# Logits in the order of use, mixing of x behind the store of a head's output, the last output tile in two halves, side copies first: a hybrid decoder layer on one core

## The chip, the cores and the metric

The kernel runs on one core of a Trainium2 chip. The metric is the device time of one execution in microseconds (us), taken as the median of several runs. Beside it stands one execution recorded by the hardware profiler, from which the profile's numbers come.

## The reference

A decoder layer over 512 positions plus 16 learned meta positions, model width 2048. One input projection gives queries, keys and values of 8 attention heads (128 wide each) and the three inputs b, c, u of a gated short convolution (1024 channels). The two groups are normalized, projected together and added to the residual; then comes a SwiGLU feed-forward part of width 5632.

```python
n = _rmsnorm(h, g_mix[l])
p = n @ w_in[l]
q, k, v, gb, gc, u = jnp.split(p, ...)
q = _rmsnorm(q.reshape(b, L, N_ATTN_HEADS, HEAD_DIM), g_q[l])
k = _rmsnorm(k.reshape(b, L, N_ATTN_HEADS, HEAD_DIM), g_k[l])
o_attn = _stick_breaking_attention(q, k, v)
o_conv = gb * _causal_dwconv(gc * u, conv_w[l])
o = jnp.concatenate([_rmsnorm(o_attn, ...), _rmsnorm(o_conv, ...)], axis=-1)
h = h + o @ w_out[l]
n2 = _rmsnorm(h, g_ffn[l])
h = h + (jax.nn.silu(n2 @ w_gate[l]) * (n2 @ w_up[l])) @ w_down[l]
```

Stick-breaking attention takes, for query t and key s, the weight beta[t,s] times the product of (1 − beta[t,j]) over the keys j between s and t, with beta = sigmoid(q·k/√128). In log space that is a reverse cumulative sum over the keys.

## The kernel before

**Products.** Every product is done in split numbers. A weight tile of 128 × 1024 is loaded into `sw_in` by the load queue of SyncE, its rounded part `hi` is cast by ScalarE (ACT, L202) and the rest `lo` is subtracted by VectorE (DVE, L203), both into one of three rotating buffers of `sw_split`. The activations are split the same way. Each product is then three matmuls on TensorE (PE): `hi·ah`, `hi·al`, `lo·ah` (L311 to L313 in the heads, L772 to L774 in the output projection, L793 to L795 in the convolution, gate/up and down).

**Stages by the span's time.** 0 to 43: start and split of x. 43 to 390: eight heads of about 42.6 us, each with the products of v, q and k. 390 to 640: products of the convolution group. 640 to 774: output projection, 16 tiles of 128 output channels over 512 positions, each with a part from attention (bank x) and a part from the convolution (bank z). 774 to 1617: 44 pairs of gate/up. 1617 to 2045: down projection.

**Work hung on the products.** A head's attention is issued in pieces between the products of the next head, by a count of finished weight steps: `after(n, work)`. `attend` makes the transposes of v (`va`, `vb`, L548 and L549), the logits z for three blocks of keys (`z_0`, `z_1`, `z_2`, L563 to L565, with two small fp32 products L568 and L569 for the last keys in `z_2`), and their logarithms on ACT and DVE (L590 to L594), with causal selects on GpSimd (POOL, L581). The sums over later keys follow in the order block 2, 1, 0 (`sums`, tiles `c`, L618 to L624; `sph`/`spl` and `bh`/`bl` are the split operands). `mix` multiplies the weights by v into `o`, writes o's split into a stage tile `st_o` (L655 and L656) and stores it by POOL's queue (L658), and adds o² to `acc_a` (L343 and L344). Small PSUM tiles (`va`, `vb`, z, c, the norms' sums) come from one pool of four banks; stage tiles from a pool of two.

`mix_x` prepares data for the convolution part: of x, loaded as four position blocks, it makes sums and differences (L477 to L482), splits them into two stage tiles `st_x` (L324) and stores them (L486). It is issued once a head, behind the split of the head's query.

**Pairs.** The convolution group, gate/up and down multiply pairs of weight tiles with position halves by a scheme of seven block products instead of eight (`pair_product`): banks x, z, y, and side copies `p1`, `p5`, `u2` of banks on ACT (L813, L815, L817) that free the bank for the next block. Sums of weight tiles for the mixed products are made on DVE (L209, L219, L252). For gate/up, the activations' mixes `f` and their splits are made from `src` behind the output tiles (`mixed_blocks`, L980 to L987). The first gate/up pair starts with the y block.

**Order.** The order of the instructions of each engine is set by a list scheduler in the order of the program text, with priorities (`high_priority`) and explicit constraints (`issue_after`, `keep_in_program_order`).

Of the kernel before, what the change touches and what calls it, by code (L numbers as in the profile page):

```python
# [15 lines left out]
P = 128  # L16
# [17 lines left out]
def hybrid_layer(ctx: ExitStack, tc: tile.TileContext, xT, w_in, w_out, w_gu, w_down, vecs, out):  # L34
# [291 lines left out]
    def rsqrt(dst, v, n, y=None, t=None, eng=ve, times=None):  # L326

        y = t512(n, "r", 3) if y is None else y
        t = t512(n, "r", 3) if t is None else t
        sc.activation(y[:, :n], v, AF.Ln)  # L330
        sc.activation(y[:, :n], y[:, :n], AF.Exp, scale=-0.5)
        sc.activation(t[:, :n], y[:, :n], AF.Square)
        if times is not None:
            eng.tensor_tensor(y[:, :n], y[:, :n], times, ALU.mult)
        eng.scalar_tensor_tensor(t[:, :n], t[:, :n], -0.5, v, ALU.mult, ALU.mult)
        eng.scalar_tensor_tensor(dst, t[:, :n], 1.5, y[:, :n], ALU.add, ALU.mult)

    def square_sum(acc, src, first, s=None, eng=gp):
# [148 lines left out]

    def qk_norm(read, dst, parts_of, name, then=None):

# [6 lines left out]
        def finish():  # L496
# [19 lines left out]
    def head(h):  # L516
# [27 lines left out]
    def attend(h, kn, kh, kl, qn, qh, ql, vt):  # L544
# [12 lines left out]

        zs = []
        for b in range(3):
            z = small(f"z{h}_{b}")  # L560
            kk, q0 = slice(b * P, (b + 1) * P), Q0[b]
# [3 lines left out]
            pe.matmul(z[:, :n], kl[:, kk], qh[:, q0:], start=False, stop=True)  # L565
# [77 lines left out]
        def mix(ws):  # L643
# [10 lines left out]
            st = stage(f"st_o{h}")[:, : 2 * SEQ].rearrange("p (a b) -> p a b", a=2)  # L654
            sc.activation(st[:, 0], o, AF.Copy, scale=g)  # L655
            ve.scalar_tensor_tensor(st[:, 1], o, g, st[:, 0].bitcast(F32), ALU.mult, ALU.subtract)  # L656
            square_sum(acc_a, o, h == 0)
            gp.dma_start(oa_dram[h], st)  # L658

        after(14, lambda: sums(2))  # L660
# [4 lines left out]
    def token_scale(acc, dst, count, name, work, eng=ve, in_order=False):  # L665
# [11 lines left out]
        ve.tensor_scalar(v, ps, 1.0 / count, EPS, ALU.mult, ALU.add)  # L677
        rsqrt(dst, v, SEQ, y, t, eng)

# [87 lines left out]

    def wide_product(ps, acts):
        hi, lo = next_w()
        for n, (k, ah, al) in enumerate(acts):  # L770
            kk = slice(k * P, (k + 1) * P)
            pe.matmul(ps, hi[:, kk], ah, start=n == 0, stop=False)  # L772
            pe.matmul(ps, hi[:, kk], al, start=False, stop=False)
            pe.matmul(ps, lo[:, kk], ah, start=False, stop=n == 7)  # L774
            tick()

# [20 lines left out]
    def pair_product(acts, cols, out2, side, fourth=None):  # L797
# [14 lines left out]
        block_product(x, acts[0], True)  # L812
        sc.copy(p1, x)  # L813
        block_product(z, acts[1], True)
        sc.copy(p5, z)  # L815
        block_product(x, acts[2], False)
        sc.copy(u2, x)  # L817
        block_product(z, acts[3], False)
# [100 lines left out]
    def out_tile():  # L919
        i = len(ps_out)  # L920
        ps_out.append([xyz.tile([P, 512], F32, tag=t, name=f"po{i}{t}") for t in ("x", "z")])

# [6 lines left out]
    for i, j in enumerate(OUT_TILES):  # L929
# [40 lines left out]
        def residual(eng):  # L970
            ve.tensor_tensor(t1, ps[0], acc_a, ALU.mult)
            eng.tensor_tensor(hj, hj, t1, ALU.add)
            ve.tensor_tensor(t2, ps[1], acc_c, ALU.mult)
            eng.tensor_tensor(hj, hj, t2, ALU.add)
            sc.activation(src[:, 2 * half : 2 * half + 2], two(hj), AF.Copy, scale=g_ffn[:, j : j + 1])

        def split_f(s, i):
            split(acts[s][:, 0, k], acts[s][:, 1, k], src[:, i])

        def mixed_blocks():  # L980
            split_f(0, 0)
            ve.tensor_tensor(src[:, 4], src[:, 3], src[:, 1], ALU.subtract)
            split_f(1, 4)
            ve.scalar_tensor_tensor(src[:, 4], src[:, 4], -1.0, src[:, 0], ALU.mult, ALU.subtract)
# [247 lines left out]
```

## Time and profile before

| | |
|---|---|
| runs | 2044.81, 2046.19, 2046.81 us; median 2046.19 |
| profiled execution | 2046.62 us, of which 2044.8 are the span |
| busy: PE, DVE, ACT, POOL | 2027.8, 1728.4, 1074.9, 349.3 us |
| mean granted clock of PE | 0.999 |
| matmuls on PE | 16134 |

A row of the timeline gives start, duration, engine, line, operation, output and input tiles, shape, number, and in square brackets the idle time ahead of it with what ended it. A row of the waits gives the engine and tile that waited, what for, the total, the number of times and the longest. A row of the stages gives their bounds and length, the busy time and the number of instructions of PE, PEld (weight loads), DVE, ACT and POOL, then the clock granted to PE (1 is full), the busy share of the DMA engines and their rate. "From start to start" means the time between two matmuls' starts, less what the same shape takes without a wait.

### The profile page before, as it was taken

How to read it: one execution, taken by the hardware profiler on the slowest of the kernel's cores; microseconds unless marked ns; L12 is line 12 of the kernel's file. 1: busy time of each engine (PE TensorE's matmuls, PEld its weight loads, DVE VectorE, ACT ScalarE, POOL GpSimd, SP SyncE). 2: the span in 40 equal slices, each digit the busy share in tenths (PEclk: the TensorE clock that was granted, in tenths of full speed). 3: DMA queues.
4: the chain of work that ended last, by engine and by line, in shares of the span. 5: the costliest groups of instructions: out<-in, count | busy, mean ns of one | idle time of the engine just before them, and what ended most of it. 6: DMA issues, size and time to landing. Idle time of an engine off the chain costs nothing.

```text
span 2044.8 us, 39586 instructions
## 1 busy us (share of the span) xinstructions
PE 2027.8 (99%) x16134; PEld 1962.6 (96%) x16134; DVE 1728.4 (85%) x2187; ACT 1074.9 (53%) x1555; POOL 349.3 (17%) x514
## 2 busy tenths in 40 slices
PE   9999999999999999999999999999999999999999
PEld 8899999899998888999999999999999999999999
DVE  7877677698887778998988988988988978888887
ACT  7766667444454435555555554555555544444443
POOL 0111112200004441011111111111111242131211
PEclk9999999999999999999999999999999999999999
DMA  6343334732355555456465465455455899797764
GB/s 220 105 134 117 122 114 152 268 119 94 114 191 176 172 162 194 142 176 182 138 176 169 133 174 171 136 172 167 141 175 161 271 342 349 171 314 199 214 154 90
DMA packets 156086, 356.28 MB, mean 174 GB/s; under 512 B 13632, under 2 KB 67648, under 8 KB 155136
## 3 DMA queue, kind: packets, MB, share of 16 engines
q1 hardware_dynamic: 72208, 216.76, 32.6%
q0 software_dynamic: 83696, 136.99, 25.0%
q8 instruction: 126, 2.06, 0.4%
q14 instruction: 56, 0.46, 0.1%
HBM read 275.78 MB, written 77.92 MB: 173 GB/s over the span
## 4 chain that ended last, share of the span: by engine, by line
PE 89%; DVE 4%; ACT 2%; DMA 2%; issue 1%; POOL 1%; SPq 0%; DVEq 0%; ACTq 0%
PE x L793 13%; PE x L795 13%; PE x L794 13%; PE z L794 6%; PE z L795 6%; PE z L793 6%; PE y L795 3%; PE y L793 3%; PE y L794 3%; DVE sw_split L203 2%; PE pv L311 1%; PE pv L312 1%; PE pv L313 1%; PE pq L313 1%; PE pq L312 1%
## 5 line engine op out<-in xcount | busy, mean ns | idle before, releaser
L202 ACT CAST sw_split<-sw_in 128x1024 fp32r<-128x1024 f32 (+2 forms) x668 | 661.5, 992 | 712.1 <-PE z L794 189.0
L203 DVE TENSOR_TENSOR sw_split<-sw_in,sw_split 128x1024 fp32r<-128x1024 f32 (+2 forms) x668 | 778.0, 1165 | 150.2 <-ACT sw_split L202 144.7
L793 PE MATMUL x<-f,sw_split 128*128 128x256 f32 x1408 | 388.3, 276 | 2.9 <-ACT sides L813 1.9
L795 PE MATMUL x<-f,sw_split 128*128 128x256 f32 x1408 | 388.2, 276 | 0.6 <-DVE sw_split L203 0.6
L794 PE MATMUL x<-f,sw_split 128*128 128x256 f32 x1408 | 388.1, 276 | 0.0
L793 PEld LDWEIGHTS x<-f,sw_split 128*128 128x128 f32 x1408 | 265.0, 188 | 3.3 <-ACT sides L813 2.1
L795 PEld LDWEIGHTS x<-f,sw_split 128*128 128x128 f32 x1408 | 265.1, 188 | 1.0 <-DVE sw_split L203 1.0
L794 PEld LDWEIGHTS x<-f,sw_split 128*128 128x128 f32 x1408 | 265.1, 188 | 0.0
L1047 POOL DMA_DIRECT2D fd<-s x147 | 103.7, 922 | 713.7 <-DVE s L324 713.0
L209 DVE TENSOR_TENSOR sw_in<-sw_in 128x1024 f32<-128x1024 f32 (+1 forms) x164 | 187.9, 1146 | 11.5 <-DMA sw_in<-w_in 3.0
L793 PE MATMUL z<-f,sw_split 128*128 128x256 f32 x704 | 193.7, 275 | 0.3 <-ACT sides L815 0.3
L794 PE MATMUL z<-f,sw_split 128*128 128x256 f32 x704 | 193.6, 275 | 0.0
L795 PE MATMUL z<-f,sw_split 128*128 128x256 f32 x704 | 193.6, 275 | 0.0
L795 PE MATMUL x<-ring,sw_split 128*128 128x256 f32 x608 | 167.3, 275 | 0.4 <-DVE sw_split L203 0.4
L793 PE MATMUL x<-ring,sw_split 128*128 128x256 f32 x608 | 167.2, 275 | 0.0
L794 PE MATMUL x<-ring,sw_split 128*128 128x256 f32 x608 | 167.2, 275 | 0.0
L793 PEld LDWEIGHTS z<-f,sw_split 128*128 128x128 f32 x704 | 132.2, 188 | 0.5 <-ACT sides L815 0.5
L794 PEld LDWEIGHTS z<-f,sw_split 128*128 128x128 f32 x704 | 132.2, 188 | 0.0
L795 PEld LDWEIGHTS z<-f,sw_split 128*128 128x128 f32 x704 | 132.2, 188 | 0.0
L795 PEld LDWEIGHTS x<-ring,sw_split 128*128 128x128 f32 x608 | 114.1, 188 | 0.6 <-DVE sw_split L203 0.6
L794 PEld LDWEIGHTS x<-ring,sw_split 128*128 128x128 f32 x608 | 114.1, 188 | 0.0
L793 PEld LDWEIGHTS x<-ring,sw_split 128*128 128x128 f32 x608 | 114.1, 188 | 0.0
(604 smaller groups left out, 5459.2 us busy)
## 6 DMA issues: line engine op xcount, KB each, us to landing
sw_in<-w_gu SPq DMA_DIRECT2D x176, 512.0 KB, 3.9
sw_in<-w_in SPq DMA_DIRECT2D x92, 512.0 KB, 3.3
fd<-s POOLq DMA_DIRECT2D x147, 256.0 KB, 5.3
sw_in<-w_down SPq DMA_DIRECT2D x96, 384.0 KB, 4.2
ring<-fd POOLq DMA_DIRECT2D x42, 768.0 KB, 16.8
sw_in<-w_out SPq DMA_DIRECT2D x32, 512.0 KB, 3.4
out_T<-d POOLq DMA_DIRECT2D x54, 256.0 KB, 5.2
mix_dram<-st_x POOLq DMA_DIRECT2D x16, 516.0 KB, 4.0
```

The costliest lines, as they stand in the source:

```text
L202: sc.copy(hi, src)
L203: ve.tensor_tensor(lo, src, hi.bitcast(F32), ALU.subtract)
L209: return ve.tensor_tensor(sums[name], a, b, ALU.add)
L311: pe.matmul(ps, wh, ah[:, a:b], start=k + i == 0, stop=False)
L312: pe.matmul(ps, wh, al[:, a:b], start=False, stop=False)
L313: pe.matmul(ps, wl, ah[:, a:b], start=False, stop=k + i == last)
L793: pe.matmul(p, hi[:, kk], ah, start=start and j == k == 0, stop=False, skip_group_check=skip)
L794: pe.matmul(p, hi[:, kk], al, start=False, stop=False, skip_group_check=skip)
L795: pe.matmul(p, lo[:, kk], ah, start=False, stop=k == n - 1, skip_group_check=skip)
L1047: gp.dma_start(fd[c][s][:, :, k], t[:, :, i])
```

## The change

1. `attend` builds the logits in the order 2, 1, 0, in which `sums` uses them, the two fp32 products right behind z_2.
2. `mix_x` of a head is issued in `mix`, behind the split of the head's output, rather than behind the split of the next head's query. The add of o² to `acc_a` goes from POOL to DVE.
3. The convolution part of the last output tile is made in two halves of positions: 256 to 511 first in bank y, then 0 to 255 in bank z. Residual and mixes follow by halves; the square sum `acc_h` comes behind the last splits.
4. The side copies of the first two pairs of the convolution and of gate/up get the highest priority (`read_out`). The table for silu is loaded right behind the last square of the feed-forward norm.

```diff
-    def qk_norm(read, dst, parts_of, name, then=None):
+    def qk_norm(read, dst, parts_of, name):
...
-            last = split(hi, lo, dst[:, :n])
-            if then:
-                with tc.issue_after(last[0].ins), tc.issue_after(last[1].ins):
-                    then()
+            split(hi, lo, dst[:, :n])
...
-        after(9 if h else 22, qk_norm(read, qn, (qh, ql, SEQ), f"q{h}", (lambda: mix_x(h - 1)) if h else None))
+        after(9 if h else 22, qk_norm(read, qn, (qh, ql, SEQ), f"q{h}"))
...
-        zs = []
-        for b in range(3):
-            z = small(f"z{h}_{b}")
+        zs = {}
+        for b in (2, 1, 0):
+            zs[b] = z = small(f"z{h}_{b}")
...
-            zs.append(z)
-        z = zs[2]
-        pe.matmul(z[:, 272:416], kn[:, 384:512], qn[:, 368:], start=True, stop=True)
-        pe.matmul(z[:, 416:432], kn[:, 512:640], qn[:, 496:], start=True, stop=True)
+            if b == 2:
+                pe.matmul(z[:, 272:416], kn[:, 384:512], qn[:, 368:], start=True, stop=True)
+                pe.matmul(z[:, 416:432], kn[:, 512:640], qn[:, 496:], start=True, stop=True)
...
-            square_sum(acc_a, o, h == 0)
+            square_sum(acc_a, o, h == 0, eng=ve)
             gp.dma_start(oa_dram[h], st)
+            if h < HEADS - 1:
+                with tc.issue_after(hi.ins), tc.issue_after(lo.ins):
+                    mix_x(h)
...
-    def wide_product(ps, acts):
+    def wide_product(parts, acts):
         hi, lo = next_w()
-        for n, (k, ah, al) in enumerate(acts):
-            kk = slice(k * P, (k + 1) * P)
-            pe.matmul(ps, hi[:, kk], ah, start=n == 0, stop=False)
...
+        for ps, a, b in parts:
+            for n, (k, ah, al) in enumerate(acts):
+                kk = slice(k * P, (k + 1) * P)
+                pe.matmul(ps, hi[:, kk], ah[:, a:b], start=n == 0, stop=False)
...
+        def read_out(dst, src):
+            with tc.high_priority(1 << 20 if i in (CONV, CONV + 1) else 0):
+                sc.copy(dst, src)
...
-        sc.copy(p1, x)
+        read_out(p1, x)
...
+        if i == KT - 1:
+            z, y = ps_out[i][1][0][0], xyz.tile([P, 512], F32, tag="y", name=f"po{i}y")
+            ps_out[i][1] = [(y[:, T2:], T2, SEQ), (z[:, :T2], 0, T2)]
...
-            ve.tensor_tensor(t2, ps[1], acc_c, ALU.mult)
-            eng.tensor_tensor(hj, hj, t2, ALU.add)
-            sc.activation(src[:, 2 * half : 2 * half + 2], two(hj), AF.Copy, scale=g_ffn[:, j : j + 1])
+            for o, a, b in ps[1]:
+                ve.tensor_tensor(t2[:, a:b], o, acc_c[:, a:b], ALU.mult)
+                eng.tensor_tensor(hj[:, a:b], hj[:, a:b], t2[:, a:b], ALU.add)
+                blks = src[:, 2 * half + a // T2 : 2 * half + b // T2]
+                sc.activation(blks, hj[:, a:b].rearrange("p (a t) -> p a t", t=T2), AF.Copy, scale=g_ffn[:, j : j + 1])
+                if a:
+                    late_block()
...
+        def late_block():
+            ve.tensor_tensor(src[:, 4], src[:, 3], src[:, 1], ALU.subtract)
+            split_f(1, 4)
...
-                square_sum(acc_h, hj, False, wide_tmp("h", bufs=2), ve)
                 split_f(3, 5)
                 split_f(4, 1)
+                square_sum(acc_h, hj, False, wide_tmp("h", bufs=2), ve)
...
-            token_scale(acc_h, acc_h, D, "h", (w[:, 0], w[:, 1], a[:, 0], a[:, 1], b), ve, True)
+            last = token_scale(acc_h, acc_h, D, "h", (w[:, 0], w[:, 1], a[:, 0], a[:, 1], b), ve, True)
+            with tc.issue_after(last.ins):
+                sc.preload_act_table_set("silu_and_others")
```

Some line numbers shift: z's matmuls stand at L561 to L566 afterwards, the transposes at L546 and L547, the side copies all at L811, silu at L1078.

On PE, at the attention work of head 2 between two steps of k's product (`pk`), before:

```order
L548 MATMUL va_2097<-ident,tmp_2055 128x128 x4
L549 MATMUL vb_2098<-ident,tmp_2055 16x128
L563 MATMUL z_0_2111<-qh_1898,kh_1768 128x512
L564 MATMUL z_0_2111<-ql_1899,kh_1768 128x512
L565 MATMUL z_0_2111<-qh_1898,kl_1769 128x512
L311 MATMUL pk_2057<-n_132,sw_split 128x272
L563 MATMUL z_1_2115<-qh_1898,kh_1768 128x400
L564 MATMUL z_1_2115<-ql_1899,kh_1768 128x400
L565 MATMUL z_1_2115<-qh_1898,kl_1769 128x400
L312 MATMUL pk_2057<-n_132,sw_split 128x272
L313 MATMUL pk_2057<-n_132,sw_split 128x272
L563 MATMUL z_2_2119<-qh_1898,kh_1768 128x272
```

and afterwards:

```order
L546 MATMUL va_2097<-ident,tmp_2055 128x128 x4
L547 MATMUL vb_2098<-ident,tmp_2055 16x128
L561 MATMUL z_2_2111<-qh_1898,kh_1768 128x272
L562 MATMUL z_2_2111<-ql_1899,kh_1768 128x272
L563 MATMUL z_2_2111<-qh_1898,kl_1769 128x272
L565 MATMUL z_2_2111<-qn_1897,kn_451 128x144
L566 MATMUL z_2_2111<-qn_1897,kn_451 128x16
L561 MATMUL z_1_2117<-qh_1898,kh_1768 128x400
L562 MATMUL z_1_2117<-ql_1899,kh_1768 128x400
L563 MATMUL z_1_2117<-qh_1898,kl_1769 128x400
L311 MATMUL pk_2057<-n_132,sw_split 128x272
L312 MATMUL pk_2057<-n_132,sw_split 128x272
```

The whole of z_2 moves ahead of z_1; z_0 follows behind the last row shown. Before, z_1's bank was that of vb; afterwards z_0's bank is that of va.

On POOL, the same head's stores and selects (`sp`, `lw`: z's logarithms and weights), before:

```order
L486 DMA mix_dram<-st_x_2_1986 128x2x516
L486 DMA mix_dram<-st_x_0_1990 128x2x516
L581 AFFINE_SELECT sp_2126<-sp_2126 128x112
L611 MEMSET lw_2125 1x112
L658 DMA oa_dram_475<-st_o_2018 128x1024
L344 TENSOR_TENSOR acc_a<-acc_a,tmp_2021 128x512
L581 AFFINE_SELECT sp_2126<-sp_2126 128x128 x2
```

and afterwards:

```order
L655 DMA oa_dram_475<-st_o_2004 128x1024
L487 DMA mix_dram<-st_x_2_2017 128x2x516
L487 DMA mix_dram<-st_x_0_2021 128x2x516
L578 AFFINE_SELECT sp_2126<-sp_2126 128x128 x2
L578 AFFINE_SELECT sp_2126<-sp_2126 128x16
```

The store of o goes ahead of the two stores of x's mix, the add of the squares is gone from POOL, and the selects of z_2 come first.

On DVE, behind the last output tile (`po15z`, `po15y`: banks of its convolution part; `src`, `f`: the activations' mixes; `sw_in` with L209 and L252: sums of weight tiles), before:

```order
L973 TENSOR_TENSOR sw_in<-po15z,acc_c 128x512
L974 TENSOR_TENSOR w_7870<-w_7870,sw_in 128x512
L203 TENSOR_TENSOR sw_split<-sw_in,sw_split 128x1024
L982 TENSOR_TENSOR src_7853<-src_7853 128x256
L344 TENSOR_TENSOR acc_h<-acc_h,w_7887 128x512
```

and afterwards:

```order
L983 TENSOR_TENSOR sw_in<-po15z,acc_c 128x256
L984 TENSOR_TENSOR w_7895<-w_7895,sw_in 128x256
L209 TENSOR_TENSOR sw_in<-sw_in 128x1024
L1001 SCALAR_TENSOR_TENSOR src_7878<-src_7878 128x256
L324 TENSOR_TENSOR f_6615<-src_7878,f_6615 128x256
L1003 SCALAR_TENSOR_TENSOR src_7878<-src_7878 128x256
L324 TENSOR_TENSOR f_6617<-src_7878,f_6617 128x256
L1004 TENSOR_TENSOR src_7878<-src_7878 128x256
L324 TENSOR_TENSOR f_6614<-src_7878,f_6614 128x256
L345 TENSOR_TENSOR acc_h<-acc_h,w_7919 128x512
L324 TENSOR_TENSOR f_7874<-src_7878,f_7874 128x256
L203 TENSOR_TENSOR sw_split<-sw_in,sw_split 128x1024
```

The weight split L203 moves behind the mixes, and L209 ahead of them.

On ACT, around the end of the first gate/up pair (L1057, later L1076: copy of the gate out of its bank), before:

```order
L1057 COPY g_7927<-x_7931 128x256
L202 CAST sw_split<-sw_in 128x1024 x2
L1059 ACT_TABLE_LOAD
L1059 ACTIVATE g_7927<-g_7927 128x512
L202 CAST sw_split<-sw_in 128x1024
L813 COPY sides<-x_8161 128x256
L815 COPY sides<-z_8160 128x256
```

and afterwards:

```order
L332 ACTIVATE work_b<-work_a 128x512
L1050 ACT_TABLE_LOAD
L202 CAST sw_split<-sw_in 128x1024 x2
L811 COPY sides<-x_8190 128x256
L1076 COPY g_7955<-x_7959 128x256
L202 CAST sw_split<-sw_in 128x1024 x2
L811 COPY sides<-z_8189 128x256
L1078 ACTIVATE g_7955<-g_7955 128x512
```

The table load moves up behind the norm, and the two side copies stand ahead of silu.

More of the change, by code (lines that the diff above doesn't have):

```diff
@@ L331, in rsqrt @@
         sc.activation(y[:, :n], y[:, :n], AF.Exp, scale=-0.5)
-        sc.activation(t[:, :n], y[:, :n], AF.Square)
+        last = sc.activation(t[:, :n], y[:, :n], AF.Square)
         if times is not None:
@@ L336, in rsqrt @@
         eng.scalar_tensor_tensor(dst, t[:, :n], 1.5, y[:, :n], ALU.add, ALU.mult)
+        return last
     def square_sum(acc, src, first, s=None, eng=gp):
@@ L677, in token_scale @@
         ve.tensor_scalar(v, ps, 1.0 / count, EPS, ALU.mult, ALU.add)
-        rsqrt(dst, v, SEQ, y, t, eng)
+        return rsqrt(dst, v, SEQ, y, t, eng)
     def cu_product(name):
@@ L766, in hybrid_layer @@
     sides_c = ctmp.tile([P, 3, N], F32, name="sides_c")
[L768 removed]
+    def wide_product(parts, acts):
         hi, lo = next_w()
[L770 to L775 removed]
+        for ps, a, b in parts:
+            for n, (k, ah, al) in enumerate(acts):
+                kk = slice(k * P, (k + 1) * P)
+                pe.matmul(ps, hi[:, kk], ah[:, a:b], start=n == 0, stop=False)
+                pe.matmul(ps, hi[:, kk], al[:, a:b], start=False, stop=False)
+                pe.matmul(ps, lo[:, kk], ah[:, a:b], start=False, stop=n == 7)
+                if b == SEQ:
+                    tick()
     def block_product(ps, act, start):
@@ L812, in pair_product @@
         block_product(x, acts[0], True)
-        sc.copy(p1, x)
+        read_out(p1, x)
         block_product(z, acts[1], True)
-        sc.copy(p5, z)
+        read_out(p5, z)
         block_product(x, acts[2], False)
-        sc.copy(u2, x)
+        read_out(u2, x)
         block_product(z, acts[3], False)
@@ L920, in out_tile @@
         i = len(ps_out)
-        ps_out.append([xyz.tile([P, 512], F32, tag=t, name=f"po{i}{t}") for t in ("x", "z")])
+        ps_out.append([[(xyz.tile([P, 512], F32, tag=t, name=f"po{i}{t}"), 0, SEQ)] for t in ("x", "z")])
+        if i == KT - 1:
+            z, y = ps_out[i][1][0][0], xyz.tile([P, 512], F32, tag="y", name=f"po{i}y")
+            ps_out[i][1] = [(y[:, T2:], T2, SEQ), (z[:, :T2], 0, T2)]
     after(3, scale_c)
```

10 lines of the change are left out of this document (5 added, 5 removed).

## The prediction

> **What bounds the kernel now.** I read the page's busy shares first.
>
> ```profile
> PE 2027.8 (99%) x16134; PEld 1962.6 (96%) x16134; DVE 1728.4 (85%) x2187; ACT 1074.9 (53%) x1555; POOL 349.3 (17%) x514
> ```
>
> PE is the bound, and its matmuls number almost the same before and after, so the change can only win or lose time in which PE stands still or runs slowly. The profiled execution took 2046.62 us, of which 2044.8 are the span and 1.8 lie around it; the three runs have the median 2046.19, 0.4 us lower. All sums below are made against 2046.62. A measurement of this kernel tells about 0.2% from no change, 4.1 us, so "faster" begins at 2042.1 and "slower" at 2050.3.
>
> Next, the waits of PE over the whole span (total, times, longest):
>
> ```profile
> PE x L795 <- DVE sw_split L203: 2.8, 4, 1.7
> PE c L621 <- DVE bl L324: 2.1, 6, 0.4
> PE x L793 <- ACT sides L813: 1.9, 1, 1.9
> PE x L793 <- DVE u L823: 1.0, 1, 1.0
> PE c L620 <- ACT bh L324: 0.3, 1, 0.3
> ```
>
> and the same by stages (length, then busy time of PE, PEld, DVE, ACT, POOL, granted clock, DMA share, GB/s):
>
> ```profile
> 774.40:809.10 34.70, 30.92 (x243) 29.80 (x242) 31.18 (x41) 19.03 (x29) 2.41 (x4) 0.95 0.67 227
> 804.80:808.20 3.40, 3.40 (x17) 3.40 (x18) 2.96 (x4) 0.07 (x1) 0.00 (x0) 0.51 0.35 127
> ```
>
> The waits on bl and bh lie in the heads (43 to 390), those on sides L813 and on u in the passage from the output projection to gate/up (774 to 809); these are the two places the change touches. The last row is the only stretch at half clock, and it stands right behind the wait of 1.9 us on sides. The longest wait of the first row, 1.7, is at the first conv pair (413), which the change leaves alone.
>
> **The change, part by part.**
>
> *Order of the logits, and mixing behind the head's output (43 to 390).* PE's rows at one head:
>
> ```profile
> 178.14 0.28 PE L311 MATMUL pk<-n,sw_split 128*128 128x272 f32 x1
> 178.51 0.45 PE L563 MATMUL z<-qh,kh 128*128 128x400 f32 x1
> 178.80 0.34 PE L564 MATMUL z<-ql,kh 128*128 128x400 f32 x1
> 178.98 0.35 PE L565 MATMUL z<-qh,kl 128*128 128x400 f32 x1
> 179.16 0.29 PE L312 MATMUL pk<-n,sw_split 128*128 128x272 f32 x1
> 179.29 0.29 PE L313 MATMUL pk<-n,sw_split 128*128 128x272 f32 x1
> ```
>
> A 272-column matmul starts the next one 0.13 us later (179.16 to 179.29), a 400-column one 0.18 later (178.80 to 178.98). The first z1 matmul starts 0.37 behind its predecessor, so 0.24 late, and itself takes 0.29 to the next, 0.11 too much, as the first matmul behind a stall does elsewhere. No wait is listed for it because the modelled ends overlap. It waits for the PSUM slot of vb, which DVE frees late:
>
> ```profile
> 178.19 0.27 DVE L555 COPY v<-vb 16x128 f32<-16x128 f32 x1
> 178.85 0.27 DVE L554 COPY v<-va 128x128 f32<-128x128 f32 x1
> ```
>
> Price: 0.35 a head, in seven of eight heads, 2.5 us. After the change the slot is taken by z0, the last of the three, and the one it takes is va's. From va and vb on, PE then has z2 (three matmuls at 0.13, the two diagonal ones 0.4), z1 (three at 0.18), two pk matmuls: z0 is due at about 179.0. The copy of va comes behind the split of x's mix as before; with the mix ahead of it finishing some 0.3 us earlier (below), va is free at about 178.8. So I take the whole 2.5; the other end is nothing won, if the copy stays at its 179.12.
>
> The second loss is in the sums, eleven us later:
>
> ```profile
> 189.88 0.36 PE L618 MATMUL c<-sph,later_r 128*128 128x432 f32 x1
> 190.28 0.29 PE L620 MATMUL c<-bh,ones_r 128*128 128x288 f32 x1
> 190.94 0.40 PE L621 MATMUL c<-bl,ones_r 128*128 128x288 f32 x1 [0.36 <-DVE bl L324]
> 191.18 0.39 PE L311 MATMUL pq<-n,sw_split 128*128 128x512 f32 x1
> ```
>
> With 288 columns L621 was due 0.13 behind L620 and comes 0.53 late, and the next matmul 0.11 more: 0.63 a head, six heads, 3.8 us. Head 0 has a like wait of L620 (the last row of the waits), 0.6 with its restart. Why bl is late, from the chain:
>
> ```profile
> 183.68 0.74 DVE L656 SCALAR_TENSOR_TENSOR st_o<-o,vec,st_o 128x512 fp32r<-128x512 f32 x1
> 184.72 0.56 POOL L658 DMA_DIRECT2D oa_dram<-st_o  x1 [2.47 <-DVE st_o L656]
> 185.30 1.32 POOL L344 TENSOR_TENSOR acc_a<-acc_a,tmp 128x512 f32<-128x512 f32 x1
> 186.55 1.16 POOL L581 TENSOR_SCALAR_AFFINE_SELECT sp<-sp 128x128 f32<-128x128 f32 x3
> 187.75 0.55 ACT L324 CAST sph<-sp 128x432 fp32r<-128x432 f32 x1 [2.15 <-POOL sp L581]
> ```
>
> The causal selects of z2 stand on POOL behind the store of the previous head's output and behind the add of its squares. Two edits clear this: z2 is made first, so its sp is ready some 3 us earlier, and the output's split and store go ahead of x's mix, while the add (1.32 us of POOL, seven times) becomes one of DVE (0.69 by L334's 512 columns). By hand on before's durations: sp of z2 at 180.5, selects to 182.3, bl done near 185, 5 us before L621 needs it. I take 3.8 and 0.6; a bound below that needs the whole slack lost.
>
> What pays for it: DVE gets the output's split (0.74) and the add (0.69) between 169.6 and 173.5, where it had 2.0 us idle ahead of 168.97:
>
> ```profile
> 168.50 0.39 PE L652 MATMUL o<-lw,v 16*128 16x16 f32 x2
> 168.97 0.69 DVE L334 TENSOR_TENSOR tmp<-tmp,tmp 128x512 f32<-128x512 f32 x1 [2.02 <-ACT tmp L332]
> 171.02 0.62 ACT L324 CAST qh<-qn 128x512 fp32r<-128x512 f32 x1 [2.09 <-DVE qn L336]
> 176.31 1.15 ACT L324 CAST st_x<-x_mix 128x516 fp32r<-128x516 f32 x2 [2.48 <-issue]
> ```
>
> The output o is complete at about 168.9, and ACT stood idle for 2.09 us ahead of 171.02, then 2.48 ahead of the cast of x's mix. So the cast and the square of o go into ACT's gaps, DVE shifts ql and the copy of v by about a microsecond, and the cast of the mix comes at about 176.0 instead of 176.31. None of these is waited for by PE before 177. Cover for all of it: the pv and pk products, 9 us without a wait. **Heads: 2.5 + 3.8 + 0.6 = 6.9 us won**; other end 3.0 won (z's wait stays, half of a like wait in c comes back).
>
> *The new wait of the same edit.* The pool of stage tiles has two buffers. The output's tile st_o is now followed by the mix's two tiles, so the second of these takes st_o's buffer and its cast on ACT must wait until the store of st_o has landed. Behind that cast on ACT stand vh and the logits' first reads, on DVE vl and the copy that frees va, and PE's z0 waits for that. The store is issued at about 171.2, the cast is due at 176.6, and z0 begins to suffer when the store takes over 5.7 us. What it took before, over eight heads, and the other store of this pool by the page:
>
> ```profile
> DMA to landing us min/median/max: 3.1/5.5/7.3
> ```
>
> ```profile
> mix_dram<-st_x POOLq DMA_DIRECT2D x16, 516.0 KB, 4.0
> ```
>
> But those stores left near 185, and the new ones leave at 171:
>
> ```profile
> 171.00:177.00 6.00, 6.00 (x52) 6.00 (x51) 4.10 (x8) 3.50 (x6) 0.00 (x0) 1.00 0.10 20
> ...
> 184.00:191.00 7.00, 6.64 (x44) 5.86 (x42) 6.38 (x13) 4.85 (x11) 3.53 (x8) 1.00 0.75 224
> ```
>
> With a DMA share of 0.10 instead of 0.75 I take 4 us, nearest the other store, and cost nothing; at 7.3, the other end, it is a rival below.
>
> *Last output tile in halves, side copies first, silu's table ahead (774 to 809).* The 24 conv matmuls of 512 columns become 48 of 256; gate/up's 256-column matmuls follow each other at 0.113 and the 512s at 0.227, so nothing is added. Before, the stage from 774.4 to 809.1 holds ten blocks of 24 such matmuls and two of 512: 27.65 us of 34.70, so 7.05 are lost. The listed waits of 1.9 and 1.0 are its two largest stalls, 2.06 and 1.14 from start to start; 3.40 us at clock 0.51 give away 1.7; three small stalls of 0.4 to 0.55 and the restarts are the rest. What the two largest hang on:
>
> ```profile
> 793.77 1.23 DVE L209 TENSOR_TENSOR sw_in<-sw_in 128x1024 f32<-128x1024 f32 x1 [1.26 <-DMA sw_in<-w_gu]
> ```
>
> ```profile
> 801.46 1.28 ACT L1059 ACT_TABLE_LOAD   x1
> 802.76 0.63 ACT L1059 ACTIVATE g<-g 128x512 f32<-128x512 f32 x1
> ```
>
> The 2.06 goes: the side copy that PE waited for stood on ACT behind the table load, silu and a cast; now it stands ahead of silu, and the table is loaded behind rsqrt. The 1.14 goes too: L209 on DVE waited for a load, and u behind it; in the new order the addition that frees that load's buffer comes some 8 us earlier. But the order of DVE after the last output tile brings a new one:
>
> ```profile
> 774.58 0.69 DVE L973 TENSOR_TENSOR sw_in<-po15z,acc_c 128x512 f32<-128x512 f32 x1 [1.48 <-PE po15z L774]
> 775.91 1.22 DVE L203 TENSOR_TENSOR sw_split<-sw_in,sw_split 128x1024 fp32r<-128x1024 f32 x1
> 777.05 0.42 DVE L982 TENSOR_TENSOR src<-src 128x256 f32<-128x256 f32 x1
> ```
>
> The weight split at 775.91 serves the third matmul of the first z block, which is due behind the 48 of y and x and two more, 774.4 + 50 × 0.113 = 780.05. In the new order it stands behind the second half's residual (two of 0.42), L209 (1.22), six mixing operations and splits of 0.42, the square sum (0.69) and one more split; neighbours overlap by about 0.08. From 775.7, where the second half's product is multiplied, this comes to a start at 780.7 and an end at 781.9: PE stalls 1.87. ACT's casts, which wait for that block, then push the copy of bank z, 1.43 more; 0.2, 0.25 (a cast behind the table load) and 0.7 follow. These are sums of the rows' durations in the new order, estimates good to half a microsecond each. With restarts of 0.6 the loss is 5.1 instead of 7.05: **1.95 won**. Bounds: 4 won (the 1.87 comes out as half a microsecond and the 1.43 behind it as little) to 1.5 lost (the 1.43 doubles, and a clock drop).
>
> The granted clock decides 1.7 us here. The listed wait of 1.9 was followed by 3.4 us at 0.51; that of 1.7 at the conv products was not:
>
> ```profile
> 413.00:417.00 4.00, 3.77 (x30) 3.65 (x31) 3.66 (x6) 0.91 (x1) 0.00 (x0) 1.00 0.34 127
> ```
>
> A stall of 1.87 from start to start would be listed, in the measure of these (2.06 is listed as 1.9), as 1.7, like the latter, so I take full clock. The Trainium skill, "TensorE: Matmul & The Clock Gate", Part 1, says that the clock halves after at least one idle window of about 3.4 us. This trace disagrees about the length, since a wait of 1.9 us was followed by half clock; by the page's rule no stall here could halve it, and the sum would be the one I give. The same skill, "ScalarE: Activation LUTs", What ACT_TABLE_LOAD costs, counts some 2.7 us with the drain; the row shows 1.28 and silu 0.02 behind it. By the page ACT would be 1.4 later behind the early load, and the sum would be 1.4 higher.
>
> *Elsewhere.* The order on PE and on the load queue stays, so the 2.7 us lost at the first conv pair and the tail stay: nothing.
>
> **Sum.** 2046.62 − 6.9 − 1.95 = 2037.8 us.
>
> **The rivals.**
>
> *Half clock after the new stall* (like 804.8, unlike 413): 1.7 back, 2039.5. Chance 0.10.
>
> *The passage gives nothing or loses up to 1.5*, because DVE's new order costs more than the two old stalls: 2039.7 to 2041.3. For it: DVE is busy 31.2 of 34.7 us there, so it hides nothing. Chance 0.10.
>
> *The wait of z only moves to z0*, since the copy of va ended at 179.12 before the change, after the 179.0 at which z0 is due: 2040.3. Chance 0.07.
>
> *Heads won only in part or not at all* (another late operand at L618, which stands 0.4 ahead of L621): 2042.1 to 2046.6. This includes that the change does not do what it says. Chance 0.16.
>
> *Slower: the store of st_o holds the mix.* At 7.3 us to landing the cast starts 1.9 late instead of 0.3 early for z0: PE stalls 1.6 and 0.1 for its restart in each of seven heads, 11.9 us, with z's 2.5 not won: 2046.62 − 3.8 − 0.6 − 1.95 + 11.9 = 2052.2. It decides from 5.7 us on, and at about 7.0 the whole change turns slower. For it: the median 5.5 is close. Against: the quiet queue. Chance 0.11.
>
> **How the numbers follow.** The forecast has 0.46. Faster is the forecast and the first three rivals, 0.73; same 0.16; slower 0.11. The range runs from 2036.0 (the passage's better bound) to 2046.3; below it I leave 0.05, above it the slower case and a little of the case before it.
>
> **What would show it.** Right: no wait of c for bl, z's first matmuls 0.13 or 0.18 behind their predecessors, POOL's selects within 2 us of sp, the store landing in under 5 us, no ACT_TABLE_LOAD in front of a side copy, and one stall of about 1.9 us on the z block near 780 at full clock. Wrong: ACT idle ahead of the cast of st_x for DMA, z0 waiting for a slot, or a stretch at half clock near 782.

## The result and the profile after

The changed kernel takes 2037.65 us (median of 6 runs, 2036.67 to 2039.69), the kernel before, run beside it, 2045.67 (2044.81 to 2046.81): a ratio of 0.9962, 95% interval 0.9952 to 0.9973. The profiled execution took 2037.97 us with a span of 2036.1. The forecast was 2037.8.

The page's busy shares of the changed kernel: 24 matmuls more, 5 us less of busy time on PE (in part because the stretch at half clock is gone, where 17 matmuls kept PE busy for 3.4 us), and 11 us less on POOL.

```profile
PE 2022.7 (99%) x16158; PEld 1962.6 (96%) x16158; DVE 1728.1 (85%) x2196; ACT 1078.8 (53%) x1556; POOL 337.9 (17%) x507
```

To compare kernels I use one measure: the **time PE lost**, which is the time between two neighbouring matmuls' starts less what their shape takes, summed over all neighbours where it is above 0.06 us. It sees stalls that the list of waits does not show, and half clock too. By it the heads lost 15.5 us before and 8.3 after, the passage from the output projection to gate/up 6.8 before and 5.1 after; all other stages stayed within half a microsecond.

*The heads.* PE's waits in the heads, all of them in the changed kernel:

```profile
PE ss_q L502 <- DVE sl_q L324: 0.2, 1, 0.2
```

The waits of c for bl and bh are gone. On the timeline of PE at the same head as in the prediction, the two places where it had stood still:

```profile
176.54 0.29 PE L311 MATMUL pk<-n,sw_split 128*128 128x272 f32 x1
176.66 0.29 PE L312 MATMUL pk<-n,sw_split 128*128 128x272 f32 x1
176.79 0.39 PE L561 MATMUL z<-qh,kh 128*128 128x512 f32 x1
177.02 0.39 PE L562 MATMUL z<-ql,kh 128*128 128x512 f32 x1
...
187.62 0.29 PE L617 MATMUL c<-bh,ones_r 128*128 128x288 f32 x1
187.75 0.30 PE L618 MATMUL c<-bl,ones_r 128*128 128x288 f32 x1
187.88 0.39 PE L311 MATMUL pq<-n,sw_split 128*128 128x512 f32 x1
```

Each matmul now starts 0.12 to 0.13 us behind the last one of 272 or 288 columns. What they wait for, on DVE and POOL:

```profile
176.22 0.28 DVE L552 COPY v<-va 128x128 f32<-128x128 f32 x1
181.70 0.45 DVE L324 TENSOR_TENSOR bl<-lw,bh 128x288 fp32r<-128x288 f32 x1
```

```profile
168.92 0.56 POOL L655 DMA_DIRECT2D oa_dram<-st_o  x1 [10.85 <-DVE st_o L653]
175.38 1.40 POOL L487 DMA_DIRECT2D mix_dram<-st_x  x2 [5.90 <-DVE st_x L324]
178.88 0.68 POOL L578 TENSOR_SCALAR_AFFINE_SELECT sp<-sp 128x128 f32<-128x128 f32 x3 [2.10 <-PE pk L313]
```

The copy that frees va's bank ends at 176.50, 0.29 ahead of z0's start; bl ends at 182.15, 5.6 ahead of its use. POOL makes z2's selects at 178.88, after 2.10 us without work.

*The store that the mix could wait for.* The landing of the head's output, over eight heads, and the two rows of ACT's waits in the heads that name it:

```profile
DMA to landing us min/median/max: 2.9/3.1/5.4
```

```profile
ACT st_x L324 <- DMA oa_dram<-st_o: 0.3, 1, 0.3
ACT acc_hi L324 <- DMA oa_dram<-st_o: 0.2, 1, 0.2
```

ACT's casts of the mix waited once, for 0.3 us (the other row is the sum of squares behind the last head); none of PE's z matmuls behind them came late.

*The passage.* From the first y matmul to the fourth block of the second pair it took 34.7 us before; now (767.35 to 800.41) it takes 33.1, and the clock is whole:

```profile
767.40:800.40 33.00, 29.23 (x243) 28.00 (x243) 28.82 (x38) 19.05 (x30) 2.80 (x4) 1.00 0.69 237
```

PE's waits there, and its rows at the two longest:

```profile
PE z L797 <- DVE sw_split L203: 1.7, 1, 1.7
PE z L795 <- ACT sides L811: 1.3, 1, 1.3
PE x L797 <- DVE sw_split L203: 0.4, 1, 0.4
PE z L795 <- ACT sw_split L202: 0.2, 1, 0.2
```

```profile
772.96 0.28 PE L796 MATMUL z<-f,sw_split 128*128 128x256 f32 x1
774.98 0.39 PE L797 MATMUL z<-f,sw_split 128*128 128x256 f32 x1 [1.74 <-DVE sw_split L203]
...
777.50 0.28 PE L797 MATMUL z<-f,sw_split 128*128 128x256 f32 x1
779.07 0.39 PE L795 MATMUL z<-f,sw_split 128*128 128x256 f32 x1 [1.29 <-ACT sides L811]
```

From start to start these are 1.90 and 1.45 us. The first is the weight split behind the mixes on DVE, which ends at 774.92:

```profile
773.71 1.21 DVE L203 TENSOR_TENSOR sw_split<-sw_in,sw_split 128x1024 fp32r<-128x1024 f32 x1
```

The second is a choice of ACT's order:

```profile
777.70 1.04 ACT L202 CAST sw_split<-sw_in 128x1024 fp32r<-128x1024 f32 x1 [2.32 <-PE z L796]
778.65 0.37 ACT L811 COPY sides<-z 128x256 f32<-128x256 f32 x1
```

The cast needs the z block's last use of `hi`, one matmul ahead of the block's end; the side copy needs the end. The cast stands first and begins 0.08 ahead of that end (777.78), so the copy starts 0.87 behind it, and PE waits for the copy.

### The profile page after: what moved, and what is told of

Read it like the earlier page. It is cut to its first block, busy times and chain, and to the rows that moved or that the text cites. A ratio compares the mean times of both kernels' runs of the same rounds, so it can differ in the third digit from the quotient of the medians.

```text
span 2036.1 us, 39674 instructions
## 1 busy us (share of the span) xinstructions
PE 2022.7 (99%) x16158; PEld 1962.6 (96%) x16158; DVE 1728.1 (85%) x2196; ACT 1078.8 (53%) x1556; POOL 337.9 (17%) x507
## 4 chain that ended last, share of the span: by engine, by line
PE 92%; DVE 3%; DMA 2%; ACT 1%; issue 1%; POOL 0%; SPq 0%; DVEq 0%; ACTq 0%; POOLq 0%
PE x L795 13%; PE x L797 13%; PE x L796 13%; PE z L795 7%; PE z L796 7%; PE z L797 7%; PE y L796 3%; PE y L797 3%; PE y L795 3%; PE pv L311 2%; PE pv L312 2%; PE pv L313 2%; PE pk L312 1%; PE pk L311 1%; PE pk L313 1%; PE pq L313 1%
## 5 line engine op out<-in xcount | busy, mean ns | idle before, releaser
L203 DVE TENSOR_TENSOR sw_split<-sw_in,sw_split 128x1024 fp32r<-128x1024 f32 (+2 forms) x668 | 777.8, 1165 | 149.2 <-ACT sw_split L202 144.3
L209 DVE TENSOR_TENSOR sw_in<-sw_in 128x1024 f32<-128x1024 f32 (+1 forms) x164 | 187.9, 1146 | 13.1 <-DMA sw_in<-w_in 5.0
```

The lines of the kernel that those rows point to most:

```text
L203: ve.tensor_tensor(lo, src, hi.bitcast(F32), ALU.subtract)
L209: return ve.tensor_tensor(sums[name], a, b, ALU.add)
```

## The experiments

Times are medians; "heads" and "passage" are the time PE lost there in the profiled execution. Each ratio is to the runs of the kernel before that were made beside that kernel (their medians lie between 2045.39 and 2046.00), not to the first row. The kernel before once more is a single execution.

| kernel | us | ratio to before, 95% interval | heads | passage |
|---|---|---|---|---|
| before, and once more | 2046.19, 2046.35 | | 15.5, 15.4 | 6.8, 6.8 |
| changed, and once more | 2037.65, 2036.53 | 0.9962 [0.9952, 0.9973], 0.9956 [0.9944, 0.9969] | 8.3, 8.4 | 5.1, 4.3 |
| z_order | 2039.07 | 0.9965 [0.9951, 0.9979] | 10.0 | 6.5 |
| mix_late | 2039.27 | 0.9967 [0.9954, 0.9980] | 9.7 | 4.7 |
| acc_dve | 2041.38 | 0.9980 [0.9971, 0.9989] | 11.5 | 5.1 |
| halves | 2048.35 | 1.0008 [0.9998, 1.0017] | 15.6 | 8.2 |
| copies | 2043.01 | 0.9987 [0.9978, 0.9996] | 15.6 | 3.2 |
| no_halves, and once more | 2035.47, 2035.12 | 0.9951 [0.9934, 0.9969], 0.9948 [0.9934, 0.9962] | 8.2, 8.5 | 3.2, 2.5 |
| t1_copy | 2036.31 | 0.9954 [0.9938, 0.9970] | 8.4 | 3.6 |
| after_nopre | 2037.23 | 0.9961 [0.9946, 0.9976] | 8.2 | 4.9 |
| store_slow | 2039.45 | 0.9973 [0.9964, 0.9983] | 8.3 | 4.8 |

**The heads: which edit frees bl?** Three kernels, each the kernel before with one part of the change.

z_order, the logits' order alone:

```diff
-        for b in range(3):
+        for b in (2, 1, 0):
```

> The kernel before with the logits' order 2, 1, 0 alone; mixing of x, store and add of squares stay where they were. Theory (the late operand bl comes from the selects of z2 on POOL): with z2 first its sp is ready before the previous head's output reaches POOL, so the wait of c for bl goes although store and add still stand on POOL: 3.8 + 0.6 us won. The wait for vb's bank stays at z1 (0.35 a head), since the copy of vb still comes behind the mix: about 2042.2 beside a before of 2046.6, PE lost in the heads (starts later than the shapes' cadence) 15.5 before, about 11 here. Rival (the store and the add on POOL are what makes bl late): the wait of c stays at 0.3 to 0.5 a head, only z's wait may go: 2044 to 2046.

The waits of c for bl and bh are gone, as the theory has it. The kernel is faster than expected, 2039.07 against 2042.2: the heads lost 10.0 us and not 11, and the expectation started from 2046.6, while the kernel before took 2045.42 beside it. The wait for vb's bank stays at z1, shorter than before, on PE's timeline 0.18 late (177.17 behind 176.86):

```profile
176.86 0.37 PE L311 MATMUL pk<-n,sw_split 128*128 128x272 f32 x1
177.17 0.45 PE L563 MATMUL z<-qh,kh 128*128 128x400 f32 x1
```

mix_late, only the mixing behind the store and the add of the squares on DVE:

```diff
-        after(9 if h else 22, qk_norm(..., (lambda: mix_x(h - 1)) if h else None))
+        after(9 if h else 22, qk_norm(...))
...
+            square_sum(acc_a, o, h == 0, eng=ve)
+            if h < HEADS - 1:
+                with tc.issue_after(hi.ins), tc.issue_after(lo.ins):
+                    mix_x(h)
```

> The kernel before with only the mixing of x behind the store of the head's output, and the add of squares on DVE; logits in the order 0, 1, 2. Theory: POOL is free when z2's sp comes, so bl is in time even with z2 last (3.8 + 0.6 won), and z1 gets another bank than vb's (2.5 won): about 6.5 won, 2040. Rival (z2 first is what is needed): c still waits for bl 0.3 or more a head, 2043 to 2044. Third: the store of st_o holds the cast of the mix (ACT waits for DMA), z2 stalls: above 2046.

The six waits for bl are gone here too, and behind head 0 no z is late by more than 0.13, though the logits run 0, 1, 2; only head 0 still waits for bh. So either part alone is enough for bl, and their gains overlap: 5.5 and 5.8 us in the heads, 7.2 together.

acc_dve goes one step further down, to a single instruction of mix_late:

```diff
-            square_sum(acc_a, o, h == 0)
+            square_sum(acc_a, o, h == 0, eng=ve)
```

> The kernel before with a single edit: the add of the squares of a head's output on DVE (0.69) rather than on POOL (1.32); mixing and logits as before. Theory (any of the things that stand ahead of z2's selects on POOL is enough to make bl late, and bl is late by only 0.5): the selects come 1.3 earlier, bl about 0.5 earlier, since DVE has the add to do now: the wait of c shrinks from 0.5 to 0.0 to 0.2 a head, 3 to 4 us won, 2042 to 2043. Rival (the place of the store, or z2 being last, is what counts): the wait of c stays, no change.

Its POOL, with the store still ahead of the selects, then its bl on DVE and its sums on PE:

```profile
183.72 0.56 POOL L658 DMA_DIRECT2D oa_dram<-st_o  x1 [2.47 <-DVE st_o L656]
184.50 1.30 POOL L581 TENSOR_SCALAR_AFFINE_SELECT sp<-sp 128x128 f32<-128x128 f32 x4 [0.21 <-DVE sp L593]
```

```profile
188.71 0.45 DVE L324 TENSOR_TENSOR bl<-lw,bh 128x288 fp32r<-128x288 f32 x1
```

```profile
189.28 0.29 PE L620 MATMUL c<-bh,ones_r 128*128 128x288 f32 x1
189.41 0.30 PE L621 MATMUL c<-bl,ones_r 128*128 128x288 f32 x1
```

The selects start 0.78 behind the store's issue instead of 1.83, bl is ready 0.25 ahead of its use, and all six stalls are gone: 4.0 us of the heads' loss for one add on another engine. Of the edits tried it is the smallest that carries this term. PE's wait for vb's bank stays, 0.24 at z1 in six heads.

**The passage: halves or copies?** Again the kernel before with one part each. halves has the last output tile in two parts with its mixes (`wide_product`, `out_tile`, `residual`, `mixed_blocks`); copies has `read_out` and the early table load.

> The kernel before with only the last output tile in two halves and its mixes. Theory (the halves bring the two new stalls of 1.90 and 1.45, the side copies' order takes the 2.06 and the half clock away): both old and new stalls here, 1.9 + 1.45 near 773 and about 2 near 802 with half clock behind it; the 0.45, 0.40, 0.54 and 1.14 of before gone. Loss in the passage 7.5 to 8.5 against 6.8 before: 0.7 to 1.7 slower than before, 2047 to 2048. Rival (the halves are what gains, by ending the residual earlier): 2 us faster than before, 2044.6.

> The kernel before with only the side copies first and silu's table behind rsqrt. Theory: the 2.06 stall and the 3.4 us at half clock behind it go (3.8 won), the stalls of 0.45, 0.40, 0.54 and 1.14 stay, a wait of about 0.4 behind the table load comes: loss in the passage about 3.5 against 6.8 before, 2043.3. Rival (the copies only move the stall to the next block, or the table load costs as much ahead of the casts as it did ahead of silu): loss stays at 6 to 7, no change from before.

PE's waits in the passage, of halves and of copies:

```profile
PE x L795 <- ACT sw_split L202: 2.0, 1, 2.0
PE x L795 <- ACT sides L815: 1.8, 1, 1.8
PE z L797 <- DVE sw_split L203: 1.6, 1, 1.6
```

```profile
PE x L794 <- DVE u L828: 1.0, 1, 1.0
PE x L796 <- DVE sw_split L203: 0.5, 1, 0.5
PE z L794 <- ACT sides L810: 0.3, 1, 0.3
```

The theory's sums hold: in the profiled executions the halves alone lose 1.4 us more than before, the copies alone 3.6 less. Of these 3.6, 1.7 is the half clock, which does not come in every execution; by the medians of the runs the copies won 2.4 us (2045.42 to 2043.01). In halves not every part came as expected. Its second stall was 2.13 us instead of 1.45, with half clock behind it, and the one near 808 was 1.93 with full clock. And by the times alone halves cannot be told from the kernel before, as its interval includes 1. So whether the change contains a part that costs time is settled by no_halves, the changed kernel without that part:

```diff
-        if i == KT - 1:
-            z, y = ps_out[i][1][0][0], xyz.tile([P, 512], F32, tag="y", name=f"po{i}y")
-            ps_out[i][1] = [(y[:, T2:], T2, SEQ), (z[:, :T2], 0, T2)]
```

> The changed kernel with the last output tile whole again (its residual, mixes and square sum as before the change); heads, side copies and table load as changed. Theory (the halves cost more than they save, 5.13 lost in the passage with them, 3.2 with the copies' order alone): heads lose 8.3 as in the changed kernel, the passage about 3.2, no stall at the first z block: 1.9 us faster than the changed kernel, 2035.7. Rival (the two parts need each other: with the whole tile the late load and the side copies stall again): passage 5 or more, no better than the changed kernel, 2037.5 to 2039.

It has the lowest median of this study. To compare it with the changed kernel on one chip, both ran once more, five runs each:

> The changed kernel once more, on the same chip as the kernel without halves, to measure the two side by side: 2037.5 to 2038; passage 5.1 lost, heads 8.3.

> The changed kernel with the last output tile whole, once more beside the changed kernel on the same chip: 1.9 faster by the loss of PE in the passage (3.2 against 5.1). Rival (the 2035.5 of the first run was that chip): no difference over 0.5 us.

2035.12 (2034.69 to 2035.40) against 2036.53 (2036.02 to 2037.44): 1.4 us faster, and the runs do not overlap. The loss in the passage was 2.5 against 4.3. The halves do win something: the stall of 1.14 for u is gone with them, while no_halves keeps it with 1.20 and 0.53 us. They pay more for it with the stalls of the two z blocks. In the repeated changed kernel the first of these was 1.07 instead of 1.90, since DVE's row behind the last tile ran about 0.85 earlier against PE. Both traces lead this back to a load: ACT's cast of a weight tile waited for a tile of w_gu until 7.92 us ahead of the first y matmul in the one (759.43), 8.76 in the other (758.39), and the work of ACT and DVE on the last tiles stands behind that cast.

t1_copy mends the two stalls that the halves brought, by order:

```diff
-                split_quad(sums["t1"], n)
+                with tc.high_priority(1 << 21 if i == CONV else 0):
+                    split_quad(sums["t1"], n)
...
+            elif last_copy[0] is not None:
+                with tc.issue_after(last_copy[0].ins):
+                    prepare()
```

> The changed kernel with two edits: the split of the first z block's weights gets a higher priority than the residual's mixes, and the casts of the next weights wait for the side copy ahead of them (first two pairs). Theory (the 1.90 stall is that split's place on DVE, the 1.45 a cast of 1.05 that takes ACT 0.1 us before the side copy is ready): both go with their restarts, 3.6 us: passage loses about 1.5, 2034.1. Rival (DVE has too much to do there, so the stall moves to the x block's or the next z block's activations f): passage still 4 to 5, 2037 to 2038.

Both went, and the rival was half right: a new stall of 1.53 (1.37 by the list of waits) stands at the next block, whose weight sum now comes late on DVE, with the cast behind it on ACT. Another new one, of 1.25, stands at 806.74, also for a cast of ACT. It lies behind the passage's end but is counted in the 3.6; up to that end the loss is 2.3. The first one:

```profile
774.57 1.22 DVE L253 TENSOR_TENSOR sw_in<-sw_in 128x1024 f32<-128x1024 f32 x1
```

```profile
775.82 1.04 ACT L202 CAST sw_split<-sw_in 128x1024 fp32r<-128x1024 f32 x1 [0.51 <-DVE sw_in L253]
```

```profile
776.91 0.39 PE L801 MATMUL x<-f,sw_split 128*128 128x256 f32 x1 [1.37 <-ACT sw_split L202]
```

DVE is the scarce engine behind the last tile: here, putting one thing first put another last.

after_nopre leaves out the early load of silu's table:

```diff
-            with tc.issue_after(last.ins):
-                sc.preload_act_table_set("silu_and_others")
```

> The changed kernel without the early load of silu's table, which then stands right ahead of the first silu. Theory (the table load costs 1.28 wherever it stands, and early it holds a weight cast by 0.40 + 0.11): that stall goes, and behind the second pair's z copy nothing waits: 0.5 faster, 2037.1. Rival (ahead of silu it holds the third side copy of the second pair as it held the first one in the kernel before): a stall of 0.5 to 1.3 more, 2038 to 2039. If a load cost 2.7 with a drain, ACT would be idle 1.4 behind it.

The load then stands ahead of the first silu, ACT's rows there:

```profile
798.17 1.28 ACT L1076 ACT_TABLE_LOAD   x1
799.47 0.64 ACT L1076 ACTIVATE g<-g 128x512 f32<-128x512 f32 x1
```

The stall of 0.40 went and one of 0.75 on the lower weight part came in the same block, as DVE's and ACT's order shifted; the passage lost 4.9 against 5.1 and 4.3. With the side copies ahead of it, the table's place made no difference that these runs resolve. Silu starts 0.02 behind the load: nothing more is charged.

**Could the store have made it slower?** store_slow stores each head's output three times, so that the stage tile is read longer:

```diff
+            for n in range(2):
+                gp.dma_start(spare[n], st)
             gp.dma_start(oa_dram[h], st)
```

> The changed kernel with two more stores of each head's output to spare memory ahead of the real one, so that the stage tile is read longer. Theory (the second stage tile of x's mix waits for the store of the output, PE's z0 suffers from 5.7 us after the store's issue on): three stores of 512 KB land about 8 to 9 us after the first issue, the cast waits 2 to 3 us for DMA, z0 stalls 2 to 3 us in each of seven heads: 14 to 23 us slower than the changed kernel, 2052 to 2061. Rival (there is enough other work between, or the mix takes another buffer): no wait of z0, at most 1 us slower, 2038 to 2039.

The heads lost 8.3 as without the stores. The expectation missed because ACT's order changed with it: the cast of vh, which z0's bank hangs on, now stands ahead of the second cast of the mix (in the changed kernel both casts of the mix, at 173.73, stand ahead of vh, at 175.23).

```profile
173.13 0.62 ACT L324 CAST st_x<-x_mix 128x516 fp32r<-128x516 f32 x1 [2.32 <-DVE x_mix L484]
174.63 0.48 ACT L324 CAST vh<-va 128x384 fp32r<-128x384 f32 x1 [0.88 <-PE va L547]
175.01 0.62 ACT L324 CAST st_x<-x_mix 128x516 fp32r<-128x516 f32 x1
```

So the price of a late store in the changed kernel's own order was not tried; shown is only that its store lands in 2.9 to 5.4 us, under the 5.7 from which it would cost by the prediction's sum. The extra time of this kernel lies elsewhere: in its profiled execution (2042.43, 3.0 above its median) PE lost 8.4 us in the convolution's stage instead of 3.6, with waits of 3.05 and 1.61 for loads of `mixed` and 6.8 us at half clock behind the first.

**The clock.** The prediction took the length of a stall as the sign for half clock. The kernel before ran once more:

> The kernel before once more, for its clock. Theory (whether a stall of 2.06 us is followed by 3.4 us at half clock depends on where it falls against a window that runs freely, not on its length alone): the stall near 802 is 2.06 again, and the clock behind it may be whole; PE's loss in the passage is then 5.1 instead of 6.8. Rival (the length decides, over about 1.9 the clock halves): half clock again for 3.4 us, 6.8 lost.

The stall was 2.04 and half clock followed. But z_order, mix_late and acc_dve keep the same stall in the same place of the program, listed as 1.9, and give two answers. The 3.4 us behind it, in before_again, z_order, mix_late and acc_dve:

```profile
804.40:807.80 3.40, 3.40 (x18) 3.40 (x19) 3.07 (x4) 0.18 (x1) 0.00 (x0) 0.57 0.36 141
```

```profile
799.00:802.40 3.40, 3.40 (x18) 3.40 (x19) 3.04 (x4) 0.15 (x1) 0.00 (x0) 0.58 0.37 136
```

```profile
798.10:801.50 3.40, 3.40 (x30) 3.40 (x31) 3.06 (x4) 0.67 (x2) 0.00 (x0) 1.00 0.33 127
```

```profile
800.40:803.80 3.40, 3.40 (x29) 3.40 (x30) 3.06 (x4) 0.66 (x2) 0.00 (x0) 1.00 0.40 145
```

Stalls of 2.04 to 2.06 were followed by 17 or 18 matmuls in 3.4 us three times (the kernel before twice and z_order), by 29 or 30 twice. So length alone does not decide, and the rival falls. Executions of one kernel differ too: of 21 runs of the kernel before, made beside the first experiments, ten had a mean granted clock of 1.000 (2043.64 to 2045.42 us) and eleven a lower one (2045.29 to 2048.66).

The place of the stall fits the theory. In every trace here the granted clock changes only at whole multiples of 3.413 us from its first change; in the kernel before, from 6.15 to 804.87 is 234 of them. So an execution can be laid out in windows of that length. In the kernel before (both times) and z_order the whole stall lies in one window; in mix_late and acc_dve a window ends inside the stall, at 797.86 and at 800.25. The window that holds most of the stall, in z_order and in acc_dve:

```profile
796.14:799.55 3.41, 1.51 (x13) 1.31 (x13) 3.41 (x4) 3.00 (x5) 0.00 (x0) 1.00 0.63 186
796.83:800.25 3.42, 1.63 (x15) 1.43 (x13) 3.42 (x5) 3.39 (x6) 0.00 (x0) 1.00 0.55 164
```

PE was busy for 1.51 us of the first, and half clock came with the next window; for 1.63 us of the second, and it did not. This holds throughout: over all fourteen traces, from 43 us on, five windows at full clock had PE busy for 1.54 us or less, and half clock followed each of them (before twice, z_order, halves, store_slow); all others had 1.63 or more, and it followed none. No edit moved a stall against the windows on purpose, so this is read from the traces and not tested.

## Why the prediction was right, step by step

- **Wait of c for bl, 3.8 and 0.6 won:** right in size and in mechanism; the six waits and head 0's are gone, bl is 5.6 us early where about 5 was worked out. What it said of the cause, "two edits clear this", was too much: the order of the logits, the mixing's place with the add, and the add alone each clear the six waits.
- **Wait of z for vb's bank, 2.5 won:** right. va was free 0.29 ahead of z0 (0.2 worked out). It needs the mixing's place: with the order alone z1 still took vb's bank and was 0.18 late.
- **The heads together:** 6.9 forecast, 15.5 − 8.3 = 7.2 measured. Of these the one add on DVE alone brings 4.0.
- **The new wait for the store:** right that it costs nothing; 4 us to landing taken, 3.1 measured in the median. The longest took 5.4, above the 5 that the prediction gave as a sign. The queue was less quiet than taken: the DMA share was 0.47 where the store now leaves (168.9 to 172.0), neither the 0.10 of the prediction nor the 0.94 that it met before (184.7 to 190.2). That this is why it lands sooner is not shown.
- **The passage, 1.95 won:** 6.8 − 5.1 = 1.7 in the profiled execution, 2.5 in the second one. The stalls worked out from the order and the rows of before, 1.87, 1.43, 0.2, 0.25 and 0.7, came as 1.90, 1.45, 0.24, 0.40 and 0.59. That the 1.87 was met to 0.03 is in part luck, as the same stall was 1.07 in the second execution. Not seen was that this sum holds 3.6 won by the copies and 1.4 to 1.9 lost by the halves; the prediction named the new stall, but took the parts as one.
- **Full clock behind the 1.87 stall:** the outcome was right, the reason only in part. That a listed 1.7 does not halve the clock and a listed 1.9 does was read from one case each, and five stalls of one length gave both: where the stall lies in the window counts beside its length. A stall of 1.93 in halves, nearly all of it in one window, was still followed by full clock, with PE busy for 1.67 us there. The Trainium skill, "TensorE: Matmul & The Clock Gate", Part 1, says that the clock's window of about 3.4 us runs freely. These traces agree: the changes lie 3.413 us or a multiple of it apart, and the first one comes at another time in each execution (6.15 in before, 4.25 in z_order). Its other statement, that a whole idle window is needed, does not fit: PE was busy for 1.51 us of z_order's window.
- **The whole:** 8.85 us forecast, 8.65 between the two profiled executions, 8.0 between the medians (2045.67 and 2037.65). That the forecast meets the new median to 0.15 us is in part luck: it started from an execution 0.95 above the median of the kernel before, with 1.7 us of half clock that not every execution has.

What stays open: whether the clock would follow a stall that is moved on purpose against the windows, why the load of w_gu landed 0.84 us later against PE in one execution than in the other, and what a late store costs.

## What to carry to other kernels

Where the bound engine is busy 99% of the time, read its starts, not its busy time: the 2.5 us at z's bank stood in no list of waits. When several edits aim at one late operand, try the smallest alone; here moving one add from POOL (1.32 us) to DVE (0.69) gave 4.0 of the 7.2 us in the heads. And undo each part of a change that has won: the tile in halves, made to end the residual earlier, cost 1.4 to 1.9 us, as it filled DVE just when the next weights were to be split.

## What was not expected of the hardware

The first matmul behind a stall takes about 0.11 us longer to the next one (0.29 instead of 0.18 at 400 columns, 0.22 instead of 0.11 at 256), with the clock whole; behind stalls of over 0.2 us it was 0.10 to 0.11 in most cases, and 0.08 in some. A load of ACT's table took 1.28 us, and the next instruction on ACT, the casts at 790.25 in the changed kernel, followed at once:

```profile
788.96 1.28 ACT L1050 ACT_TABLE_LOAD   x1
790.25 2.00 ACT L202 CAST sw_split<-sw_in 128x1024 fp32r<-128x1024 f32 x2
```
